# Four heads' compressed probabilities turned by one transpose and laid on a block diagonal by GpSimd's transfers

## The chip, the core and the metric

The kernel runs on one core of a Trainium2 chip. TensorE (PE) multiplies and transposes, and writes only to PSUM; VectorE (DVE) and ScalarE (ACT) read PSUM and do the element-wise work; SyncE (SP) issues nearly all transfers; GpSimd (POOL) has three short instructions. Each engine works through its own list in order and waits for the others on semaphores. The metric is the time of one execution on the device in microseconds, the median of several runs.

## The reference

One transformer layer on 512 positions of width 1024: half a SwiGLU feed-forward, a mixer, half a SwiGLU, a last norm. Half of the mixer's heads are sliding-window heads; the other half (two groups `g` of four heads `r`) add three branches: attention to all selected blocks, to a window, and to 31 compressed blocks of 32 positions. The compressed branch, cut to what matters:

```python
kc = compress_blocks(kc_raw, ck_pos, ck_w1, ck_b1, ck_w2)
vc = compress_blocks(vc_raw, cv_pos, cv_w1, cv_b1, cv_w2)
s = einsum('btgrd,bcgd->bgrtc', q, kc) * ATTN_SCALE
s = where(mask_c, s - slopes * dist_c, NEG_INF)
p_cmp = where(mask_c, softmax(s), 0.0)
o_cmp = einsum('bgrtc,bcgd->btgrd', p_cmp, vc)
...
return g0 * o_cmp + g1 * o_slc + g2 * o_win
```

Everything is float32. The kernel splits each operand into a high part (rounded) and a low part (the rest) and multiplies the parts, so every matrix that PE reads comes as two.

## The kernel before

The attention is a list of stages (class `Swa` for the sliding heads, class `Nsa` for the others), each for one group `g`, one block `i` of 128 queries and, in `Nsa`, one branch `br`. `attend` interleaves the scores of one stage with the outputs of the stage before it, and fills in between with pieces of other work (`fillers`: projections, and from the last block on `mix_out`, the output projection, lines 216 to 218 of the PE list). A stage's scores end with the normalisation: `tensor_scalar` on the probabilities `p` (line 1127, every second or third head on ACT), and last of all `tensor_tensor` on the compressed probabilities `self.c` (line 1131), a tile of 128 queries by 4 heads by 32 blocks.

Eight of the stages have a compressed part: per group one with `br == 0` (`i == 0`, where all branches are one stage) and three with `br == 2`. They are called compressed stages 1 to 8 here, in order of time. In their outputs, `transposed` turns the probabilities of each block of 128 keys: four PE transposes (one for each head) into one PSUM bank, an ACT copy for the high part (line 996) and a DVE subtraction for the low part (line 997). `times_values` does so for two blocks ahead and multiplies the turned blocks by the values (lines 1030 and 1031, PSUM bank `pv`). The compressed part is the last piece of that list: four transposes of 128 by 32 into 32 rows, a copy and a subtraction of 32 by 512, written to rows 0 to 31 of a tile `ct` whose other rows are zero, and two matmuls against `CV`, whose rows 0 to 31 hold the compressed values of the group and whose other rows are zero. `CV` is made once, in `network_o(1)` (lines 895 and 896).

The list of each engine is not simply the order of the code: the framework places the instructions of a stage by its own estimate of when they are ready. Tiles with four or fewer buffers (PSUM's `mm`) are reused in turn. The names in the traces: `mm`, `sc`, `pv` are PSUM banks, `u` the tiles of high and low parts, `small` the tile that holds `self.c`, `cv` is `CV`.

Of the kernel before, what the change touches and what calls it, by code (L numbers as in the profile page):

```python
# [10 lines left out]
F32R = mybir.dt.float32r  # L11
BF16 = mybir.dt.bfloat16
AF = mybir.ActivationFunctionType
ALU = mybir.AluOpType
AX = mybir.AxisListType

P = 128
# [29 lines left out]
def tile_hybrid(ctx, tc, xT, f1_wi, f1_wo, wm_t, wm_n, cw1, cw2, small, wm_oa, wm_ob, wm_oc, f2_wi, f2_wo, const, out):  # L47
    nc = tc.nc
    V, A, PE = nc.vector, nc.scalar, nc.tensor

    sb = ctx.enter_context(tc.tile_pool(name="sb", bufs=1))
    psp = ctx.enter_context(tc.tile_pool(name="psp", bufs=1, space=bass.MemoryType.PSUM))

    def f(ap):
        return ap.bitcast(F32)

    def ps(tag="mm"):
        return psp.tile([P, 512], F32, tag=tag, name=tag, bufs=NB[tag])
# [8 lines left out]
    def flat(dt=F32R):  # L67
        return sb.tile([P, 1024], dt, tag="u", name="u", bufs=NU)

    def unit(dt=F32R):  # L70
        return flat(dt).rearrange("p (a t) -> p a t", a=2)
# [4 lines left out]
    def tmp():  # L76
        return sb.tile([P, 512], F32, tag="tmp", name="tmp", bufs=NTMP)
# [16 lines left out]
    ident = sb.tile([P, P], F32, tag="ident", name="ident")  # L94
# [708 lines left out]

    CV = sb.tile([P, 2, 2, HD], F32R, tag="cv", name="cv")
    ct = unit()
    zero = ones.unsqueeze(1).to_broadcast([P, 4, P])
    A.activation(CV.rearrange("p g a d -> p (g a d)").rearrange("p (a t) -> p a t", t=P), zero[:, :2], AF.Copy, scale=0.0)
    for a in range(2):  # L810
        A.activation(ct[:, a, :].rearrange("p (a t) -> p a t", t=P), zero, AF.Copy, scale=0.0)

# [57 lines left out]
    def network_o(kv):  # L870
        hT, w2 = state["hT", kv]
        po = ps()
        if kv == 0:
            for c in range(2):
                PE.matmul(po[:HD, :62], w2[:, c, :], hT[:, c, :], start=c == 0, stop=c == 1)
            kc = tmp()
            V.memset(kc[:HD, :64], 0.0)
            V.tensor_copy(
                kc[:HD, :64].rearrange("p (g c) -> p g c", g=2)[:, :, :NCMP],
                po[:HD, :62].rearrange("p (g c) -> p g c", g=2),  # L880
            )
            for g in range(2):
                put_key(kc[:HD, g * 32 : g * 32 + 32], 0, KT[g][0][:, 512:544], KT[g][1][:, 512:544])
        else:
            vc = tmp()
            V.memset(vc[:32, :128], 0.0)
            for g in range(2):
                for c in range(2):
                    PE.matmul(
                        po[:NCMP, g * HD : (g + 1) * HD], hT[:, c, g * NCMP : (g + 1) * NCMP], w2[:, c, :],  # L890
                        start=c == 0, stop=c == 1,
                    )
            V.tensor_copy(vc[:NCMP, :128], po[:NCMP, :128])
            vcv = vc[:32, :128].rearrange("p (g d) -> p g d", g=2)
            A.copy(CV[:32, :, 0, :], vcv)
            V.tensor_tensor(CV[:32, :, 1, :], vcv, f(CV[:32, :, 0, :]), op=ALU.subtract)
        yield 0.6


# [4 lines left out]
    def put_key(src, g, k1, k2):  # L904

        own = slice(g * HD, (g + 1) * HD)
        oth = slice((1 - g) * HD, (2 - g) * HD)
        A.copy(k1[own], src)
        V.tensor_tensor(k2[own], src, f(k1[own]), op=ALU.subtract)
        nc.sync.dma_start(f(k1[oth]), f(k1[own]))  # L910
        nc.sync.dma_start(f(k2[oth]), f(k2[own]))

    def keys(b, kind):
        o = ps()
        yield from proj(b, o)
        if kind == "b":
            SK.extend([unit(), unit()])
        elif not KT:
            for _ in range(2):
                k12 = double(F32R)  # L920
                KT.append([k12[:, :1056], k12[:, 1056:]])
        kz = tmp()
        V.tensor_tensor(kz, o, state["bc"], op=ALU.mult)
        for g in range(2):
            rows = slice(g * HD, (g + 1) * HD)
            if kind == "b":
                put_key(kz[rows, :], g, SK[0][:, g, :], SK[1][:, g, :])
            else:
                c = 544 if kind == "w" else 0
                put_key(kz[rows, :], g, KT[g][0][:, c : c + 512], KT[g][1][:, c : c + 512])  # L930


    VT = []
# [54 lines left out]
    def small_t(n, name):  # L988
        return sb.tile([P, n], F32, tag="st" + name, name=name, bufs=3)

    def transposed(pl, rows, cols):
        pt = ps()
        for r in range(4):
            PE.transpose(pt[:rows, r * P : (r + 1) * P], pl[r][:, cols], ident)  # L994
        u = unit() if rows == P else ct
        A.copy(u[:rows, 0, :], pt[:rows, :])
        V.tensor_tensor(u[:rows, 1, :], pt[:rows, :], f(u[:rows, 0, :]), op=ALU.subtract)
        return u

    def put_o(pv, kb0, i):  # L1000
        low = tmp()
        A.copy(low[lo, :], pv[hi, :])
        pvv = pv.rearrange("p (a two t) -> p a two t", a=2, two=2)
        lov = low.rearrange("p (a two t) -> p a two t", a=2, two=2)
        ob = tmp()[:, :256].rearrange("p (a t) -> p a t", a=2)
        for par in range(2):
            V.tensor_tensor(ob[par * HD : (par + 1) * HD], pvv[lo, :, par, :], lov[lo, :, par, :], op=ALU.add)
        ts = slice(i * P, (i + 1) * P)
        for a in range(2):
            if OB[kb0 + a] is None:  # L1010
                OB[kb0 + a] = unit()
            u = OB[kb0 + a]
            A.copy(u[:, 0, ts], ob[:, a, :])
            V.tensor_tensor(u[:, 1, ts], ob[:, a, :], f(u[:, 0, ts]), op=ALU.subtract)

    def times_values(work, pv, first, last):


        pairs = [work[n : n + 2] for n in range(0, len(work), 2)]
        ahead = []  # L1020
        for n in range(len(pairs) + 1):
            cur = []
            if n < len(pairs):
                cur = [(transposed(pl, rows, cols), rows, v) for pl, cols, rows, v in pairs[n]]
                if n == 0:
                    yield 0.44 * len(cur)
            for m, (u, rows, v) in enumerate(ahead):
                a = first and n == 1 and m == 0
                b = last and n == len(pairs) and m == len(ahead) - 1
                PE.matmul(pv, v, u[:, 0, :], start=a, stop=False)  # L1030
                PE.matmul(pv, v, u[:, 1, :], start=False, stop=b)
                yield 0.43 + 0.44 * len(cur) / len(ahead)
            ahead = cur

    class Nsa:
# [98 lines left out]
        def outputs(self):  # L1134
            g, i, br = self.g, self.i, self.br
            if br != 2:
                state["pv"] = ps("pv")
            pv = state["pv"]

            def values_of(b, kb):  # L1140
                return VT[b][:, kb, g].rearrange("p a d -> p (a d)")

            if br == 0:
                work = [(self.p, slice(b * P, (b + 1) * P), P, values_of(b, 0)) for b in range(2)]
            else:
                work = [(self.p, slice(kb * P, (kb + 1) * P), P, values_of(br - 1, kb)) for kb in range(i + 1)]
            if br != 1:
                cl = [self.c[:, r, :] for r in range(4)]
                work.append((cl, slice(0, 32), 32, CV[:, g].rearrange("p a d -> p (a d)")))
            yield from times_values(work, pv, br != 2, br != 1)  # L1150
            if br != 1:
                put_o(pv, g * 2, i)

    class Swa:
# [41 lines left out]
        def outputs(self):  # L1196
            g, i, W, c0 = self.g, self.i, self.W, self.c0
            pv = ps("pv")
            work = [
                (self.p, slice(n * P, (n + 1) * P), P, VT[2][:, c0 // P + n, g].rearrange("p a d -> p (a d)"))  # L1200
                for n in range(W // P)
            ]
            yield from times_values(work, pv, True, True)
            put_o(pv, 4 + g * 2, i)
# [68 lines left out]
    kb, vals = keys(8, "b"), values()  # L1273
# [15 lines left out]
    piece("c1", compressed(1))  # L1289
    piece("kw", keys(3, "w"))  # L1290
    piece("o0", network_o(0))
    piece("n1", network(1))
    piece("q4", queries(4))
    piece("q5", queries(5))
    piece("o1", network_o(1))
    piece("q6", queries(6))
    piece("q7", queries(7))
# [122 lines left out]
```

## Time and profile before

| | |
|---|---|
| median of 3 runs | 972.47 us (972.42 to 972.49) |
| the profiled execution | 973.86 us, its span 972.1 us |
| PE busy | 957.3 us (98%) |
| DVE busy | 814.3 us (84%) |
| ACT busy | 633.2 us (65%) |
| POOL busy | 3.5 us |

The span is the time from the first to the last recorded instruction; what lies around it is the difference to the execution's time. Matmuls are pipelined, so the recorded duration of one is longer than its distance to the next; what one costs in a dense stretch is read from the distance of starts. The compressed stages lie between about 478 and 603 us.

### The profile page before, as it was taken

To read this page: it belongs to the slowest core of one execution; us is meant where nothing else is said; L and a number is where in the kernel's file an instruction comes from. 1 tells how busy PE (TensorE), PEld (TensorE's weight loads), DVE (VectorE), ACT (ScalarE), POOL (GpSimd) and SP (SyncE) were. 2 spreads that over 40 slices of the span, in tenths; PEclk is the share of its full clock that TensorE was granted. 3 is DMA by queue.
4 is the path that set the end of the run, shared out by engine and by line. 5 is a ranking of instruction groups with operands and counts; after the bars stand their busy time and mean duration, and the time that the engine had idled before them with its cause. 6 is when DMAs were issued, how large, how long until landed. Compare 5 with 4: busy or idle time off the path is not lost.

```text
span 972.1 us, 13619 instructions
## 1 busy us (share of the span) xinstructions
PE 957.3 (98%) x5008; PEld 809.8 (83%) x5008; DVE 814.3 (84%) x1442; ACT 633.2 (65%) x1273; POOL 3.5 (0%) x7
## 2 busy tenths in 40 slices
PE   9999999999999999999999999999999999999996
PEld 7888888888888889888777888888888888888886
DVE  6999879888798675788899999999987988879864
ACT  7786676665766545554777785768667666676654
POOL 0000000000000000000000000000000000000000
PEclk9999999999999999999999999999999999999999
DMA  8133314233124313122410212223331323312122
GB/s 317 55 130 130 142 43 141 77 119 140 46 77 172 111 45 109 44 91 84 137 44 5 83 44 70 93 75 115 126 141 44 140 77 120 134 51 94 50 64 86
DMA packets 36386, 93.98 MB, mean 97 GB/s; under 512 B 4448, under 2 KB 8928, under 8 KB 36320
## 3 DMA queue, kind: packets, MB, share of 16 engines
q1 hardware_dynamic: 35648, 92.82, 27.7%
q8 instruction: 39, 0.64, 0.3%
q10 hardware_dynamic: 672, 0.30, 0.1%
q14 instruction: 27, 0.22, 0.1%
HBM read 89.40 MB, written 2.10 MB: 94 GB/s over the span
## 4 chain that ended last, share of the span: by engine, by line
PE 88%; DVE 6%; ACT 2%; DMA 2%; issue 1%; POOL 0%; SPq 0%; ACTq 0%; DVEq 0%
PE mm L352 18%; PE mm L353 9%; PE sc L352 7%; PE mm L218 4%; PE mm L216 4%; PE mm L217 4%; PE sc L353 4%; PE pv L441 4%; PE pv L443 3%; PE sc L441 3%; PE sc L442 3%; PE pv L442 3%; PE sc L443 3%; PE mm L994 2%; PE mm L850 2%; DMA t<-in_f_wi_dram 1%
## 5 line engine op out<-in xcount | busy, mean ns | idle before, releaser
L352 PE MATMUL mm<-u 128*128 128x512 f32 x760 | 273.7, 396 | 0.2 <-ACT mm L625 0.2
L353 PE MATMUL mm<-u 128*128 128x256 f32 x760 | 211.3, 279 | 0.0
L352 PEld LDWEIGHTS mm<-u 128*128 128x128 f32 x760 | 142.5, 188 | 34.6 <-DVE tmp L643 0.8
L353 PEld LDWEIGHTS mm<-u 128*128 128x128 f32 x760 | 143.2, 188 | 6.1
L352 PE MATMUL sc<-u 128*128 128x512 f32 x304 | 110.7, 396 | 0.0
L216 PE MATMUL mm<-u 128*128 128x512 f32 x220 | 87.7, 399 | 0.5 <-ACT u L104 0.5
L218 PE MATMUL mm<-u 128*128 128x512 f32 x220 | 86.4, 393 | 0.3 <-DVE u L105 0.3
L217 PE MATMUL mm<-u 128*128 128x512 f32 x220 | 86.4, 393 | 0.0
L353 PE MATMUL sc<-u 128*128 128x256 f32 x304 | 85.0, 280 | 0.0
L352 PEld LDWEIGHTS sc<-u 128*128 128x128 f32 x304 | 57.1, 188 | 13.2
L405 DVE TENSOR_TENSOR u<-tmp,u 128x512 fp32r<-128x512 f32 (+1 forms) x96 | 60.6, 641 | 8.0 <-ACT u L404 7.9
L404 ACT CAST u<-tmp 128x512 fp32r<-128x512 f32 (+1 forms) x96 | 54.7, 585 | 18.6 <-PE sc L443 13.6
L617 ACT COPY tmp<-mm 128x256 f32<-128x256 f32 x76 | 28.4, 374 | 50.5 <-PE mm L353 50.5
L353 PEld LDWEIGHTS sc<-u 128*128 128x128 f32 x304 | 57.2, 188 | 3.0
L441 PE MATMUL pv<-u 128*128 128x512 f32 x144 | 57.3, 398 | 0.0
L441 PE MATMUL sc<-u 128*128 128x512 f32 x144 | 57.1, 397 | 0.0
L443 PE MATMUL pv<-u 128*128 128x512 f32 x144 | 56.9, 395 | 0.0
L442 PE MATMUL sc<-u 128*128 128x512 f32 x144 | 56.7, 394 | 0.0
L442 PE MATMUL pv<-u 128*128 128x512 f32 x144 | 56.6, 393 | 0.0
L443 PE MATMUL sc<-u 128*128 128x512 f32 x144 | 56.2, 390 | 0.0
L330 DVE TENSOR_TENSOR u<-t,u 128x1024 fp32r<-128x1024 f32 x38 | 46.4, 1222 | 4.9 <-ACT u L327 3.0
L218 PEld LDWEIGHTS mm<-u 128*128 128x128 f32 x220 | 41.3, 188 | 9.3 <-DVE u L105 1.2
(266 smaller groups left out, 2258.5 us busy)
## 6 DMA issues: line engine op xcount, KB each, us to landing
t<-in_f_wi_dram SPq DMA_DIRECT2D x87, 512.0 KB, 4.4
tmp<-in_f_wo_dram SPq DMA_DIRECT2D x80, 256.0 KB, 4.7
t<-in_wm_t_dram SPq DMA_DIRECT2D x13, 512.0 KB, 4.3
t<-in_cw_dram SPq DMA_DIRECT2D x8, 512.0 KB, 4.3
h<-in_xT_dram SPq DMA_DIRECT2D x4, 512.0 KB, 8.1
tmp<-in_f_wo_dram SPq DMA_DIRECT2D x16, 128.0 KB, 4.3
t<-in_wm_oa_dram SPq DMA_DIRECT2D x4, 512.0 KB, 3.8
t<-in_wm_n_dram SPq DMA_DIRECT2D x4, 408.0 KB, 5.9
```

The lines of the kernel that those rows point to most:

```text
L216: PE.matmul(o, wh[:, c], xs[k][:, 0, :], start=s0, stop=False)
L217: PE.matmul(o, wh[:, c], xs[k][:, 1, :], start=False, stop=False)
L218: PE.matmul(o, wl[:, c], xs[k][:, 0, :], start=False, stop=s1)
L330: V.tensor_tensor(wl, t[:, 0:1024], f(wh), op=ALU.subtract)
L352: PE.matmul(o, w[0][:, c], x[k], start=new, stop=False, skip_group_check=not first)
L353: PE.matmul(o[:, :256], w[1][:, c], x[k][:, 0], start=False, stop=k == 3, skip_group_check=not first)
L404: A.copy(u[:, 0, :n], raw[:, :n])
L405: V.tensor_tensor(u[:, 1, :n], raw[:, :n], f(u[:, 0, :n]), op=ALU.subtract)
L441: PE.matmul(o, wh[:, c], u[:, 0, :], start=False, stop=False, skip_group_check=True)
L442: PE.matmul(o, wh[:, c], u[:, 1, :], start=False, stop=False, skip_group_check=True)
L443: PE.matmul(o, wl[:, c], u[:, 0, :], start=False, stop=q == j1 - j0 - 1, skip_group_check=True)
L617: A.copy(z, o[:, t2])
```

## The change

`transposed_c` takes the place of `transposed` for the compressed part. It turns the whole tile of 128 queries by 4 heads by 32 blocks with one PE transpose, so that head `r` comes out in rows 32 r to 32 r + 31. ACT and DVE make the two parts in one tile `cparts` of 128 by 2 by 128. Then four GpSimd transfers, one for each head, copy 32 rows of both parts to `ct`, each to its own rows and to its own 128 columns; `ct` is zero elsewhere. The matmul against `CV` thus meets each head in other rows, and `CV` gets the same 32 rows four times: three SP transfers after line 896 replace the zeroing of `CV` at the start. `transposed_c` is called where the list of work is built, before the stage's other transposes.

```diff
--- before.py
+++ after.py
@@ -803,10 +803,11 @@
 
 
 
+
     CV = sb.tile([P, 2, 2, HD], F32R, tag="cv", name="cv")
     ct = unit()
+    cparts = sb.tile([P, 2, P], F32R, tag="cparts", name="cparts")
     zero = ones.unsqueeze(1).to_broadcast([P, 4, P])
-    A.activation(CV.rearrange("p g a d -> p (g a d)").rearrange("p (a t) -> p a t", t=P), zero[:, :2], AF.Copy, scale=0.0)
     for a in range(2):
         A.activation(ct[:, a, :].rearrange("p (a t) -> p a t", t=P), zero, AF.Copy, scale=0.0)
 
@@ -894,6 +895,8 @@
             vcv = vc[:32, :128].rearrange("p (g d) -> p g d", g=2)
             A.copy(CV[:32, :, 0, :], vcv)
             V.tensor_tensor(CV[:32, :, 1, :], vcv, f(CV[:32, :, 0, :]), op=ALU.subtract)
+            for r in range(1, 4):
+                nc.sync.dma_start(f(CV[r * 32 : r * 32 + 32]), f(CV[:32]))
         yield 0.6
 
 
@@ -988,14 +991,26 @@
     def small_t(n, name):
         return sb.tile([P, n], F32, tag="st" + name, name=name, bufs=3)
 
-    def transposed(pl, rows, cols):
+    def transposed(pl, cols):
         pt = ps()
         for r in range(4):
-            PE.transpose(pt[:rows, r * P : (r + 1) * P], pl[r][:, cols], ident)
-        u = unit() if rows == P else ct
-        A.copy(u[:rows, 0, :], pt[:rows, :])
-        V.tensor_tensor(u[:rows, 1, :], pt[:rows, :], f(u[:rows, 0, :]), op=ALU.subtract)
+            PE.transpose(pt[:, r * P : (r + 1) * P], pl[r][:, cols], ident)
+        u = unit()
+        A.copy(u[:, 0, :], pt)
+        V.tensor_tensor(u[:, 1, :], pt, f(u[:, 0, :]), op=ALU.subtract)
         return u
+
+    def transposed_c(c):
+
+        pt = ps()[:, :P]
+        PE.transpose(pt, c.rearrange("p r c -> p (r c)"), ident)
+        u = cparts
+        A.copy(u[:, 0, :], pt)
+        V.tensor_tensor(u[:, 1, :], pt, f(u[:, 0, :]), op=ALU.subtract)
+        for r in range(4):
+            rows = slice(r * 32, r * 32 + 32)
+            nc.gpsimd.dma_start(f(ct[rows, :, r * P : (r + 1) * P]), f(u[rows]))
+        return ct
 
     def put_o(pv, kb0, i):
         low = tmp()
@@ -1021,10 +1036,10 @@
         for n in range(len(pairs) + 1):
             cur = []
             if n < len(pairs):
-                cur = [(transposed(pl, rows, cols), rows, v) for pl, cols, rows, v in pairs[n]]
+                cur = [(pl if cols is None else transposed(pl, cols), v) for pl, cols, v in pairs[n]]
                 if n == 0:
                     yield 0.44 * len(cur)
-            for m, (u, rows, v) in enumerate(ahead):
+            for m, (u, v) in enumerate(ahead):
                 a = first and n == 1 and m == 0
                 b = last and n == len(pairs) and m == len(ahead) - 1
                 PE.matmul(pv, v, u[:, 0, :], start=a, stop=False)
@@ -1141,12 +1156,11 @@
                 return VT[b][:, kb, g].rearrange("p a d -> p (a d)")
 
             if br == 0:
-                work = [(self.p, slice(b * P, (b + 1) * P), P, values_of(b, 0)) for b in range(2)]
+                work = [(self.p, slice(b * P, (b + 1) * P), values_of(b, 0)) for b in range(2)]
             else:
-                work = [(self.p, slice(kb * P, (kb + 1) * P), P, values_of(br - 1, kb)) for kb in range(i + 1)]
+                work = [(self.p, slice(kb * P, (kb + 1) * P), values_of(br - 1, kb)) for kb in range(i + 1)]
             if br != 1:
-                cl = [self.c[:, r, :] for r in range(4)]
-                work.append((cl, slice(0, 32), 32, CV[:, g].rearrange("p a d -> p (a d)")))
+                work.append((transposed_c(self.c), None, CV[:, g].rearrange("p a d -> p (a d)")))
             yield from times_values(work, pv, br != 2, br != 1)
             if br != 1:
                 put_o(pv, g * 2, i)
@@ -1197,7 +1211,7 @@
             g, i, W, c0 = self.g, self.i, self.W, self.c0
             pv = ps("pv")
             work = [
-                (self.p, slice(n * P, (n + 1) * P), P, VT[2][:, c0 // P + n, g].rearrange("p a d -> p (a d)"))
+                (self.p, slice(n * P, (n + 1) * P), VT[2][:, c0 // P + n, g].rearrange("p a d -> p (a d)"))
                 for n in range(W // P)
             ]
             yield from times_values(work, pv, True, True)
```

How the PE list changes around compressed stage 2 (`g` 0, `i` 1, `br` 2): from the stage's first transposes to its matmul against `cv`. `small_3277` is the tile of compressed probabilities. Before:

```order
L216 MATMUL mm<-u 128x512
L994 MATMUL mm<-ident,tmp 128x128 x8
L994 MATMUL mm<-ident,small_3277 32x128 x4
L985 MATMUL sc<-t_3949,u 128x416
L986 MATMUL sc<-t_3949,u 128x416
L1030 MATMUL pv<-u 128x512
...
L1030 MATMUL pv<-u 128x512
L985 MATMUL sc<-t_3949,u 128x416
L1031 MATMUL pv<-u 128x512
L1030 MATMUL pv<-u,cv 128x512
L986 MATMUL sc<-t_3949,u 128x416
```

And now, where lines 997, 1006, 1045 and 1046 are the old 994, 994, 1030 and 1031:

```order
L218 MATMUL mm<-u 128x512
L1006 MATMUL mm<-ident,small_3277 128x128
L997 MATMUL mm<-ident,tmp 128x128 x8
L988 MATMUL sc<-t_3949,u 128x416
...
L1079 MATMUL sc<-u 128x32
L1076 MATMUL sc<-u 128x384
L997 MATMUL mm<-ident,tmp 128x128 x3
L1045 MATMUL pv<-u,cv 128x512
L1046 MATMUL pv<-u,cv 128x512
```

One transpose stands ahead of the eight others in place of four behind them; three transposes of the next stage and all scores have moved ahead of the matmul against `cv`.

The DVE list of the same stage, from the normalisation of the compressed probabilities on, before:

```order
L1131 TENSOR_TENSOR small_3277<-small_3277,su 128x128
L978 TENSOR_TENSOR u<-tmp,u 64x512
L105 TENSOR_TENSOR u<-t_4351,u 128x1024
L1057 TENSOR_REDUCE nm<-sc 128x1
L997 TENSOR_TENSOR u<-mm,u 128x512 x2
L1057 TENSOR_REDUCE nm<-sc 128x1
L997 TENSOR_TENSOR u<-mm,u 32x512
```

And now (line 1009 is the subtraction in `transposed_c`):

```order
L1146 TENSOR_TENSOR small_3277<-small_3277,su 128x128
L981 TENSOR_TENSOR u<-tmp,u 64x512
L105 TENSOR_TENSOR u<-t_4351,u 128x1024
L1072 TENSOR_REDUCE nm<-sc 128x1
L1009 TENSOR_TENSOR cparts<-mm,cparts 128x128
L1000 TENSOR_TENSOR u<-mm,u 128x512 x2
```

The subtraction for the compressed part stands where the first subtraction of the other blocks stood, behind the same three instructions.

POOL's list now:

```order
L197 ISA
L197 TENSOR_TENSOR rcol<-rc,mhalf 128x4 x2
L1012 DMA u<-cparts 32x2x128 x32
L197 TENSOR_TENSOR rcol<-rc,mhalf 128x4
L1429 UNCONDITIONAL_BRANCH
```

The 32 transfers, four for each compressed stage, are all that stands there between the second and the third of its computing instructions.

## Rows read from the trace of the kernel before

**Rows 1.** Windows: busy time by engine, granted clock, DMA share, in three stretches:

```profile
478.00:603.00 125.00, 122.37 (x676) 101.21 (x675) 114.66 (x288) 97.70 (x295) 0.00 (x0) 1.00 0.15 52
...
966.00:968.00 2.00, 0.00 (x0) 0.00 (x0) 1.44 (x4) 1.02 (x2) 0.00 (x0) 1.00 1.01 367
968.00:970.00 2.00, 0.00 (x0) 0.00 (x0) 0.00 (x0) 0.00 (x0) 0.00 (x0) 0.77 0.69 230
```

**Rows 2.** Groups by line and shape from 478 to 603: busy, mean ns, idle before:

```profile
L997 DVE TENSOR_TENSOR u<-mm,u 128x512 fp32r<-128x512 f32 x42 | 27.7, 682 | 2.0 <-ACT u L996 1.8
...
L1127 DVE TENSOR_SCALAR tmp<-tmp,su 128x512 f32<-128x512 f32 x12 | 5.1, 482 | 0.0
...
L997 DVE TENSOR_TENSOR u<-mm,u 32x512 fp32r<-32x512 f32 x8 | 5.3, 666 | 0.0
...
L996 ACT CAST u<-mm 32x512 fp32r<-32x512 f32 x8 | 4.5, 566 | 0.5 <-PE mm L994 0.5
...
L1013 ACT CAST u<-tmp 128x128 fp32r<-128x128 f32 x16 | 4.0, 300 | 1.9 <-DVE tmp L1007 1.9
L1014 DVE TENSOR_TENSOR u<-tmp,u 128x128 fp32r<-128x128 f32 x16 | 4.0, 285 | 0.1
...
L1127 DVE TENSOR_SCALAR tmp<-tmp,su 128x256 f32<-128x256 f32 x12 | 3.5, 341 | 0.0
```

**Rows 3.** Timeline, PE: start, duration, line, tile, shape, count:

```profile
489.07 0.60 PE L994 MATMUL mm<-ident,small 128*32 128x128 f32 x4
...
522.01 0.40 PE L216 MATMUL mm<-u 128*128 128x512 f32 x1
522.24 0.39 PE L217 MATMUL mm<-u 128*128 128x512 f32 x1
```

**Rows 4.** Timeline, DVE, after the second compressed stage's normalisation:

```profile
500.94 0.28 DVE L1131 TENSOR_TENSOR small<-small,su 128x128 f32<-128x128 f32 x1
501.25 0.69 DVE L978 TENSOR_TENSOR u<-tmp,u 64x512 fp32r<-64x512 f32 x1
501.98 1.23 DVE L105 TENSOR_TENSOR u<-t,u 128x1024 fp32r<-128x1024 f32 x1
503.12 0.55 DVE L1057 TENSOR_REDUCE nm<-sc 128x1 f32<-128x384 f32 x1
503.59 1.28 DVE L997 TENSOR_TENSOR u<-mm,u 128x512 fp32r<-128x512 f32 x2
```

**Rows 5.** Timeline, DVE, the same two lines in the first and eighth stage:

```profile
488.62 0.28 DVE L1131 TENSOR_TENSOR small<-small,su 128x128 f32<-128x128 f32 x1
...
489.51 0.69 DVE L997 TENSOR_TENSOR u<-mm,u 128x512 fp32r<-128x512 f32 x1
...
594.45 0.28 DVE L1131 TENSOR_TENSOR small<-small,su 128x128 f32<-128x128 f32 x1
...
595.76 0.69 DVE L997 TENSOR_TENSOR u<-mm,u 128x512 fp32r<-128x512 f32 x1 [0.43 <-ACT u L996]
```

**Rows 6.** Timeline, POOL, two of its three computing instructions:

```profile
25.81 1.26 POOL L197 TENSOR_TENSOR rcol<-rc,mhalf 128x4 f32<-128x4 f32 x1 [25.37 <-ACT rc L194]
360.02 1.01 POOL L197 TENSOR_TENSOR rcol<-rc,mhalf 128x4 f32<-128x4 f32 x1 [332.95 <-ACT rc L194]
```

**Rows 7.** DMA issues: tile, queue, count, KB each, us from issue to landing:

```profile
u<-u SPq DMA_DIRECT2D x4, 128.0 KB, 2.3
...
tmp<-in_cw_dram SPq DMA_DIRECT2D x2, 64.0 KB, 1.9
```

**Rows 8.** Line 842: the same weight load's issue, ns min/median/max:

```profile
L842 SPq DMA_DIRECT2D tmp<-in_cw_dram x2: 327/328/328, 419.2 to 446.1; - x2
```

**Rows 9.** Tile cv: ns min/median/max, first and last start:

```profile
L1030 PE MATMUL pv<-u,cv x8: 393/395/496, 491.3 to 600.1; 128*128 128x512 f32 x8
...
L896 DVE TENSOR_TENSOR cv<-tmp,cv x1: 280/280/280, 479.3 to 479.3; 32x128 fp32r<-32x128 f32 x1
```

**Rows 10.** Timeline, SP queue, the weight loads around that time:

```profile
475.60 27.96 SPq L117 DMA_DIRECT2D t<-in_wm_oa_dram  x3
```

## The prediction

> **What bounds the kernel now.** I read the busy times first, then the windows around the compressed stages, then the groups by shape there, then the timelines of PE and DVE in single stages, and last every row on POOL and on transfers. The window from 478 to 603 us holds all eight compressed stages: PE is busy for 122.37 of 125.00 us and DVE for 114.66, ACT for 97.70, POOL for nothing [rows 1]. PE sets the end, and DVE is close behind it. So a PE instruction that disappears is worth its distance in PE's queue, and a PE instruction that must wait costs its whole wait, since everything behind it, filler work too, stands in the same queue. What PE loses now is 125.00 - 122.37 = 2.6 us in the whole stretch.
>
> **The transposes.** Each compressed stage loses three of its four small transposes. The four of a stage take 0.60 us from first start to last end, one alone 0.27, so their starts are (0.60 - 0.27) / 3 = 0.11 us apart [rows 3]. 8 stages x 3 x 0.11 = 2.6 us, all of it on PE. The one that is left has 128 columns of weights instead of 32 but the same 128 moving columns; I take it at 0.11 as well.
>
> **The copies.** ACT's 32x512 copy (566 ns) becomes one of 128x128 (300 ns), DVE's 32x512 subtraction (666 ns) one of 128x128 (285 ns) [rows 2]: 8 x 0.27 = 2.1 us less on ACT, 8 x 0.38 = 3.0 us less on DVE. Neither is the bound, so this can only shorten PE's waits. Of the 2.6 us of waits I give back half, 1.3 us; the bounds are 0 and 2.6.
>
> **Edits at nothing.** The zeroing of CV falls in the program's start, where ACT waits for the first loads. The three SP transfers that fill CV can start after 479.6 (479.3 + 0.28), and the first matmul that reads CV starts at 491.3 [rows 9]; three SP transfers of the nearest kind land in about 2.3 us each [rows 7], so some 9 us are left over. On SP they stand between weight loads, which are spread there over 27.96 us [rows 10]: nothing is queued close behind. Without that cover they would cost the first stage only.
>
> **The transfers.** This is the term that decides. Until now the low part went from DVE straight to PE. Now, between the two, POOL issues four transfers one after another, and the matmul against `cv` waits for all four. Call N the time from the end of DVE's subtraction to the landing of the fourth: a hand-over of 0.1 us, three issue distances, and the fourth's issue to landing. The trace before has no POOL transfer, so both are bounded. Issue distance: at least that of SP's cheapest, 0.33 us [rows 8]; at most that of POOL's longest instruction, 1.26 [rows 6]. The nearest row in engine is POOL's 1.01 us for an operation on only 4 columns, nearly all of it fixed cost. I take 0.8, the middle of the two ends, on POOL's side. Landing: 1.9 us (64 KB from HBM) to 2.3 (128 KB inside SBUF) on SP [rows 7]; I take 2.2, nearer to the copy inside SBUF. So N is at least 0.1 + 3 x 0.33 + 1.9 = 3.0, at most 0.1 + 3 x 1.26 + 2.3 = 6.2, and 0.1 + 2.4 + 2.2 = 4.7 in my forecast.
>
> The Trainium skill (DMA: Bandwidth & Descriptors, Anatomy of one DMA — SWDGE (gpsimd) path) gives a GpSimd transfer about 2.0 us from end to end and calls the making of its descriptors small. If the four issues cost nothing, N would be 2.1 us by it, an estimate, and the sum below would come out as the first rival does; no run here shows it.
>
> **What covers N.** PE goes on with other work between the compressed transpose and the matmul against `cv`. I counted that work in the new PE list, with 0.23 us for a matmul of 512 columns and 0.11 for a transpose [rows 3], narrower matmuls by their width: 3.2, 4.1, 5.5, 7.9, 6.2, 5.2, 5.3 and 5.0 us in stages 1 to 8. But the subtraction is not made at once. It now stands in DVE's list where the first subtraction of line 997 stood. In stage 2, DVE ends the normalisation at 500.94 + 0.28 = 501.22 and reaches that place at 503.59, behind 0.69 + 1.23 + 0.55 us of other work [rows 4]; with its own 0.28 the parts are ready 2.65 us after the transpose could start. Stage 1: 489.51 - 488.90 + 0.28 = 0.9 [rows 5]. In stage 8 the same difference is 595.76 - 594.73 = 1.0 [rows 5], but nothing stands between any more, so 0.9 again. All eight, worked out in the same way: 0.9, 2.65, 3.5, 1.55, 2.25, 1.3, 1.5, 0.9. Cover less this delay leaves 2.3, 1.45, 2.0, 6.35, 3.95, 3.9, 3.8 and 4.1 us for N.
>
> PE's wait at the matmul is N less what is left, where positive. For N = 4.7: 2.4 + 3.25 + 2.7 + 0 + 0.75 + 0.8 + 0.9 + 0.6 = 11.4 us. For N = 3.0: 0.7 + 1.55 + 1.0 = 3.3. For N = 6.2: 3.9 + 4.75 + 4.2 + 0 + 2.25 + 2.3 + 2.4 + 2.1 = 21.9. What is queued behind the waiting matmul is the next stage's transposes and scores; ACT and DVE wait for those in turn, but use the time to clear their lists. That brings the later subtractions forward: what the delays have above 0.9 adds up to 7.35 us (1.75 + 2.6 + 0.65 + 1.35 + 0.4 + 0.6), and I take a third of it back for N = 4.7, 2.5 us, half for N = 6.2, 3.7 us, and nothing for 3.0.
>
> DVE's `tensor_scalar` of line 1127 grows by (482 - 341) / 256 = 0.55 ns a column, the subtractions by (682 - 285) / 384 = 1.03 [rows 2]: line 1127 runs at twice the rate. The Trainium skill (SBUF — State Buffer, SBUF: two separate sides) says that while DVE is in such a two-port mode, GpSimd is locked out of a shared port and cannot write the descriptors of its transfers, and it advises against issuing them there; no run here shows a case of it. By that rule the three such instructions of the next stage that fall into the issue in stages 1 and 6, about 1 us in each, would add 2 us to the sum, 979.5; by the durations alone they add nothing, and I leave them out.
>
> **Sum.** -2.6 (transposes) - 1.3 (waits given back) + 11.4 (new waits) - 2.5 (lists cleared) = +5.0 us. The profiled execution took 973.86 us with a span of 972.1; 973.86 + 5.0 = 978.9. That execution is 1.4 us above the median of the runs, 972.47, so for the median I forecast 977.5 us.
>
> **Rivals.**
>
> *The transfers are hidden.* If POOL issues as fast as SP's cheapest and they land in 1.9 us, N = 3.0 and the sum is -2.6 - 1.3 + 3.3 = -0.6, 971.9; if N is under 1.5, no stage waits and it is -3.9, 968.6. For it: SP's rows [rows 7, 8], and that the scheduler put up to 7.9 us of work in between. Against it: POOL's 1.01 us for next to nothing [rows 6], and DVE's late place in stages 2 and 3 [rows 4]. It fails from about N = 3.2 on, where the new waits (0.9 + 1.75 + 1.2 = 3.9) eat the gain.
>
> *Gain and wait cancel.* N = 3.8 (issue distance 0.5, landing 2.2): 1.5 + 2.35 + 1.8 = 5.65 of waits, less 2.6, 1.3 and 0.5 for lists cleared, +1.3 us: 973.7.
>
> *The clock falls.* If the issue takes its upper bound, PE stands for up to 4.75 us at a time. The granted clock is 1.00 through the whole stretch, and at the end of the program, after PE has stopped, still 1.00 in 966 to 968 and 0.77 in 968 to 970 [rows 1]. Three waits of 3.9 to 4.75 us (stages 1 to 3) that each brought the lower level for as long as the wait would lose half of 12.85 us, 6.4, on top of 21.9 - 2.6 - 1.3 - 3.7 = 14.3: 993. Against it: it needs the upper bound first, and no wait of before is that long. [...]
>
> That the change does not do what it says I exclude: the new lists show one transpose in place of four and 32 transfers on POOL.
>
> **How the numbers follow.** Forecast 0.58, hidden 0.20, cancelled 0.16, clock 0.06. A measurement of this kernel can tell about 0.2% from no change, 1.9 us: below 970.5 is faster, above 974.4 slower. Of the hidden case's 968.6 to 971.9 I put 0.15 below 970.5 and 0.05 above. Of the cancelled case, 0.12 lies within, 0.04 above. The forecast's own range goes from 974 to 987 (972.47 + 14.3); I put 0.02 of it within. So faster 0.15, same 0.19, slower 0.66. The range of 970.0 to 986.5 holds the forecast, the cancelled case and half of the hidden one, and leaves out the clock and the far end of the hidden case.
>
> **What would show it.** Right: POOL rows of 32 transfers about 0.8 us apart; PE idle before the first matmul on `cv` in stages 1, 2 and 3 of 2 to 3 us each, put down to a DMA; none in stage 4; PE's busy time down by some 2.6 us in the small transposes and the window from 478 to 603 about 5 us longer; the rest of the program as before. Wrong: transfers 0.3 us apart, or landing under 1.5 us, would make the first rival; a clock under 1.00 between 480 and 610, the third. If PE waits for the DVE's subtraction or for a PSUM bank instead, in places that this list does not name, the cover was counted wrongly.

## The result, and the profile after

The changed kernel takes 980.87 us (median, 980.03 to 981.31) against 972.47 us (972.30 to 972.53) of the kernel before, run by turns on one chip: ratio 1.0085, 95% interval 1.0074 to 1.0097. It is slower by 8.4 us. The profiled execution took 980.87 us with a span of 978.5.

The loss lies in the mixer alone. GpSimd's `rcol` of line 197 stands once before the mixer's input and once behind the compressed stages; in the kernel before they start at 360.02 [rows 6] and 626.14, 266.1 us apart. First the row of before, then the changed kernel (timelines, POOL; start, duration, engine, line; in brackets the idle time ahead and what ended it):

```profile
626.14 1.01 POOL L197 TENSOR_TENSOR rcol<-rc,mhalf 128x4 f32<-128x4 f32 x1 [265.10 <-ACT rc L194]
```

```profile
358.73 1.01 POOL L197 TENSOR_TENSOR rcol<-rc,mhalf 128x4 f32<-128x4 f32 x1 [332.16 <-ACT rc L194]
489.00 2.39 POOL L1012 DMA_DIRECT2D u<-cparts  x4 [129.25 <-DVE cparts L1009]
505.19 2.12 POOL L1012 DMA_DIRECT2D u<-cparts  x4 [13.80 <-DVE cparts L1009]
...
632.65 1.03 POOL L197 TENSOR_TENSOR rcol<-rc,mhalf 128x4 f32<-128x4 f32 x1 [29.51 <-ACT rc L194]
```

They are 273.9 us apart, 7.8 more; the other 0.6 lie outside the recorded span, which is 2.4 us shorter than the execution here and 1.8 before. Four transfers take POOL 2.12 us. The instructions on the tile `cparts` (ns min/median/max), and the two new kinds of transfer (tile, queue, count, KB, us from issue to landing):

```profile
L1012 POOL DMA_DIRECT2D u<-cparts x32: 536/536/706, 489.0 to 602.6; - x32
L1008 ACT CAST cparts<-mm x8: 254/266/267, 488.1 to 600.1; 128x128 fp32r<-128x128 f32 x8
L1009 DVE TENSOR_TENSOR cparts<-mm,cparts x8: 279/284/292, 488.4 to 600.4; 128x128 fp32r<-128x128 f32 x8
...
DMA to landing us min/median/max: 1.7/1.7/4.4
```

```profile
u<-cparts POOLq DMA_DIRECT2D x32, 32.0 KB, 1.7
cv<-cv SPq DMA_DIRECT2D x3, 32.0 KB, 1.9
```

The windows that answer to [rows 1] (busy time of PE, PEld, DVE, ACT and POOL, granted clock, DMA share, GB/s):

```profile
478.00:603.00 125.00, 116.28 (x616) 94.33 (x615) 106.52 (x279) 89.98 (x288) 17.05 (x32) 0.99 0.16 53
505.00:510.00 5.00, 3.09 (x14) 2.14 (x14) 4.27 (x11) 1.69 (x5) 2.12 (x4) 1.00 0.70 236
600.00:605.00 5.00, 5.00 (x25) 4.68 (x24) 3.06 (x5) 3.48 (x7) 2.12 (x4) 0.66 0.12 26
```

PE now stands for 8.7 of the 125 us, where it stood for 2.6. PE, DVE and ACT all work less in the same time: none of them is fuller than before, and they wait for each other. PE's list of waits from 470 to 640 us (who waited for whom: us in total, times, longest):

```profile
PE mm L1006 <- DVE small L1146: 2.6, 3, 2.3
PE pv L1045 <- DMA u<-cparts: 1.4, 1, 1.4
PE sc L988 <- ACT tmp L1073: 1.4, 4, 0.8
PE pv L1046 <- DVE u L1000: 1.0, 3, 0.6
PE pv L1045 <- ACT u L999: 0.9, 1, 0.9
PE pv L1045 <- DVE tmp L1022: 0.7, 1, 0.7
PE pv L1045 <- issue: 0.3, 1, 0.3
PE sc L988 <- ACT small L1073: 0.2, 1, 0.2
PE mm L997 <- DVE tmp L1142: 0.2, 1, 0.2
```

Only 1.4 of these 8.7 us are put down to a transfer. The two largest single waits, in PE's timeline:

```profile
510.25 0.47 PE L1045 MATMUL pv<-u,cv 128*128 128x512 f32 x1 [1.43 <-DMA u<-cparts]
...
597.15 0.39 PE L218 MATMUL mm<-u 128*128 128x512 f32 x1
599.80 0.31 PE L1006 MATMUL mm<-ident,small 128*128 128x128 f32 x1 [2.26 <-DVE small L1146]
599.94 3.58 PE L997 MATMUL mm<-ident,tmp 128*128 128x128 f32 x16
```

The first is stage 2, where weight loads fill the DMA engines (share 0.70 in 505 to 510) and a landing takes 4.4 us. The second is stage 8: the compressed transpose, now first, waits for the normalisation. In PE's list nothing stands between `L218` and that transpose, and on DVE the normalisation stands behind a subtraction that needs the product of this same `L218` (timeline, DVE):

```profile
597.58 0.69 DVE L1229 TENSOR_TENSOR h<-mm,h 128x512 f32<-128x512 f32 x1 [0.48 <-PE mm L218]
598.18 1.27 DVE L1142 TENSOR_SCALAR tmp<-tmp,su 128x512 f32<-128x512 f32 x3
599.37 0.28 DVE L1146 TENSOR_TENSOR small<-small,su 128x128 f32<-128x128 f32 x1
```

Behind this wait the granted clock fell to the lower of its two levels, 1.2 GHz: 16 transposes took 3.58 us, where 15 distances of 0.11 [rows 3] and one duration of 0.27 (the median of `L994` before) are 1.9. That is 1.7 us more. What stayed open is how 1.4 us of landing become a loss of 8.4.

### The profile page after: what moved, and what is told of

It reads as the page before. It is cut to its first block, busy times and chain, and to the rows that moved or that the text cites. A ratio compares the mean times of both kernels' runs of the same rounds, so it can differ in the third digit from the quotient of the medians.

```text
span 978.5 us, 13659 instructions
## 1 busy us (share of the span) xinstructions
PE 958.0 (98%) x4984; PEld 809.7 (83%) x4984; DVE 812.6 (83%) x1442; ACT 630.6 (64%) x1272; POOL 21.0 (2%) x39
## 4 chain that ended last, share of the span: by engine, by line
PE 89%; DVE 6%; ACT 2%; DMA 1%; issue 1%; POOL 0%; ACTq 0%; DVEq 0%
PE mm L352 18%; PE mm L353 9%; PE sc L352 7%; PE mm L218 4%; PE mm L216 4%; PE mm L217 4%; PE sc L353 4%; PE pv L441 3%; PE pv L443 3%; PE sc L441 3%; PE sc L442 3%; PE pv L442 3%; PE sc L443 3%; PE sc L218 2%; PE sc L217 2%; PE sc L216 2%
## 5 line engine op out<-in xcount | busy, mean ns | idle before, releaser
L218 PE MATMUL mm<-u 128*128 128x512 f32 x220 | 86.2, 392 | 0.3 <-DVE u L105 0.3
L218 PEld LDWEIGHTS mm<-u 128*128 128x128 f32 x220 | 41.3, 188 | 9.2 <-DVE u L105 0.7
```

The costliest lines, as they stand in the source:

```text
L218: PE.matmul(o, wl[:, c], xs[k][:, 0, :], start=False, stop=s1)
```

## The experiments

Each was timed in turns with the kernel before on its chip (972.1 to 972.8 us there). In the diffs, `-` is the changed kernel's line, unless said. "List" is the order in which the framework lays out one engine's instructions; the profile records 4,984 of TensorE's in every kernel with one transpose. N is the prediction's time from the end of the subtraction to the last piece in its place.

**Without the transfers.** The compressed branch adds nothing here.

```
-        for r in range(4):
-            rows = slice(r * 32, r * 32 + 32)
-            nc.gpsimd.dma_start(f(ct[rows, :, r * P : (r + 1) * P]), f(u[rows]))
```

> The changed kernel without the 32 GpSimd transfers: the turned parts are made but never laid into ct, so the compressed branch adds nothing to the output; all matmuls are still made. Theory A (the transfers' landing is what costs, as predicted): the whole loss goes and the 2.6 us of transposes come out, 969 to 971 us. Theory B (the place costs: the compressed transpose stands first and waits for the normalisation, its copies stand ahead of the others'): only the 2.1 us go for which the changed kernel's PE stands at the matmul against cv, 978 to 979 us. Theory C (the clock drop behind the 2.4 us wait in stage 8 is the larger part): 1.7 us or so depend on whether that wait is still there.

971.31 us, ratio 0.9986 (0.9977 to 0.9996): 1.5 us faster than before, and just above theory A's range. So the whole loss, 9.6 us between this kernel and the changed one, comes with the transfers and what depends on them; the first place by itself does not make it.

**At the old place.** The transpose stands behind the others of its stage again, with its transfers.

```
-                work.append((transposed_c(self.c), None, CV...))     # first
+                work.append((self.c, None, CV...))                   # transposed in its turn
```

> The changed kernel with the compressed transpose back at its old place, behind the other transposes of its stage, transfers by GpSimd as now. Theory A: the cover shrinks to 2 to 3.5 us against a chain of copy, subtraction and 3.4 us of transfers, some 1.5 to 2.5 us of wait in each of eight stages, 984 to 990 us. Theory B: the waits for the normalisation and for the late copies go (5 to 6 us), the new waits at cv are the same as in A; about 980 to 984 us.

984.02 us, 1.0112 (1.0097 to 1.0127): 3 us worse than the changed kernel, at the edge of both expectations, so it does not tell A from B. Part of the 3 us is the clock, which in its profile falls further (granted 0.97 in 478 to 603, where the changed kernel has 0.99). Its waits (whole program) say DMA for 1.3 us, and more elsewhere:

```profile
PE mm L997 <- DVE tmp L1142: 5.1, 6, 1.4
...
PE pv L1045 <- DMA u<-cparts: 1.3, 1, 1.3
```

**The first place alone**, in the kernel before: its four small transposes come ahead of the others.

```
-                work.append((cl, slice(0, 32), 32, CV...))                     # line of the kernel before
+                work.append((transposed(cl, 32, slice(0, 32)), None, 32, CV...))
```

> The kernel before with only the place changed: its four small transposes, the 32x512 copy and subtraction come first in the stage instead of last; no transfers. Theory A: 972 to 973 us, as before. Theory B: PE waits for the normalisation in stages 1, 5 and 8 and for the other blocks' copies, 976 to 979 us.

974.18 us, 1.0014 (1.0005 to 1.0023). The place costs 1.4 us here (0.5 to 2.2), between the two expectations.

**Transfers issued by SP.**

```
-            nc.gpsimd.dma_start(
+            nc.sync.dma_start(
```

> The changed kernel with its 32 transfers issued by SP in place of GpSimd. SP's issue of such a transfer took 0.57 to 0.59 us (cv), landing 1.9, so N = 0.1 + 3 x 0.58 + 1.9 = 3.7 against 0.1 + 3 x 0.54 + 1.7 = 3.4 us. Theory A: about 0.3 us more in each stage that waits, and more where weight loads stand in SP's list ahead of them, 981 to 984 us. Theory B: the same as the changed kernel within 1 us, 980 to 982 us.

978.29 us, 1.0055 (1.0039 to 1.0072). That is below both expectations. An issue takes SP 592 ns (median) against POOL's 536 and the landing is 1.9 us, so N is no shorter (3.9 in most stages), and yet the kernel is 2.6 us faster than the changed one; why is open. The loss is of the same kind (PE's waits from 470 to 640 us, in the slowest of four executions, 979.88):

```profile
PE mm L1006 <- DVE small L1146: 4.0, 3, 2.3
...
PE pv L1045 <- DMA u<-cparts: 0.5, 2, 0.3
```

The longest is again the one at stage 8, with the clock falling behind it.

**No transfers, narrow pieces.** ScalarE and VectorE write the four blocks of the diagonal themselves; the rows keep their partitions, so nothing needs to cross. First at the old place, then first of the stage.

```
-            nc.gpsimd.dma_start(f(ct[rows, :, r * P : (r + 1) * P]), f(u[rows]))
+            A.copy(u[rows, 0, c], pt[rows])                                # u = ct, c = block r
+            V.tensor_tensor(u[rows, 1, c], pt[rows], f(u[rows, 0, c]), op=ALU.subtract)
```

> One transpose of the four heads, at the old place (behind the other transposes of the stage), and no transfers: eight 32x128 copies and subtractions, four on ScalarE and four on VectorE, write the blocks of the diagonal themselves. If the loss lies in the transfers (their waits and what hangs on them): 966 to 972 us, since eight pieces of some 0.25 us on two engines stand against a copy of 0.57 and a subtraction of 0.67. If the narrow pieces on ScalarE and VectorE cost as much as the transfers, since both engines are late for the value multiplications: 975 us or more.

> The same with the one transpose first of its stage. If the first place costs about what four transposes ahead of the others cost the kernel before (+1.4 us), this is 1 to 2 us above the version at the old place; if the first place is free once nothing waits for a transfer, as the version without transfers says (971.3 us), it is equal to it within 0.5 us or up to 1 us faster.

985.14 us (1.0117 to 1.0147) and 979.92 us (1.0060 to 1.0094). The first is the second branch of its expectation; the second is in neither branch of its own, as the first place is 5.2 us better here. A loss as large comes without any transfer, so a transfer is not needed for one. But the pieces have a price of their own (with the transpose first DVE is busy for 820.3 us and ACT for 638.0, in the changed kernel 812.6 and 630.6), and the pair cannot say what the transfers cost. The second kernel has the same wait at the same place, 2.3 us for the normalisation ahead of `L1006` of stage 8, and the clock falls there too: that wait needs no transfer. (Its lists are not the changed kernel's: over a hundred of TensorE's rows stand elsewhere.)

**All transfers made, none waited for.** The value multiplications of the compressed branch read `VT[0]` in place of the tile that the transfers fill.

```
-        return ct
+        return VT[0].rearrange(...)        # read in place of ct
```

> All 32 transfers are made, but the compressed branch's value multiplications read stored values (VT[0]) in place of the tile that the transfers fill, so nothing on TensorE depends on a transfer, and TensorE's list is that of the version without transfers. If the transfers cost by the wait on their landing and by the order that this dependence gives the lists: 971 to 972.5 us, as without transfers. If they cost by being there (GpSimd's issues beside VectorE, traffic beside the weight loads): 975 us or more, up to the 980.9 of the changed kernel.

971.30 us, 0.9990 (0.9980 to 0.9999), as without transfers, and the lists of TensorE, ScalarE and VectorE are those of that kernel row for row. 32 issues and 1 MB of traffic cost nothing that can be told (971.30 against 971.31 us). What costs is that TensorE depends on them.

**One transfer of four** (three heads add nothing).

```
-        for r in range(4):
+        for r in range(1):
```

> Only the first of the four transfers of a stage is made (three heads add nothing), so the last landing stands about 1.6 us earlier, 3 issues of 0.54 us; the dependence stays. If the loss is sized by the time from the subtraction to the last landing: the two direct waits (0.33 and 1.43 us) are gone and the time is 975 us or less. If the order that the dependence gives the lists costs, TensorE's list here is near that of the version without transfers and the time is 971 to 974. If any transfer that TensorE waits for costs the whole amount: 979 to 981.

973.79 us, 1.0015 (1.0005 to 1.0024), in the first two of its three ranges, so it does not tell size from order. One wait for the transfer, with the fall of the clock behind it, is enough for the 2.5 us against the kernel without transfers (timeline, PE; windows as above; the profiled execution took 974.46):

```profile
505.09 0.39 PE L218 MATMUL mm<-u 128*128 128x512 f32 x1
507.55 0.79 PE L1045 MATMUL pv<-u,cv 128*128 128x512 f32 x1 [2.06 <-DMA u<-cparts]
```

```profile
504.00:507.00 3.00, 1.48 (x8) 0.95 (x6) 2.93 (x9) 0.67 (x2) 0.00 (x0) 1.00 0.82 320
507.00:511.00 4.00, 3.46 (x13) 3.15 (x14) 1.25 (x5) 2.17 (x6) 0.00 (x0) 0.57 0.00 0
```

It is stage 2 again: with 320 GB/s on the way, weights nearly all of it, this landing takes 4.1 us where six others take 1.7 to 1.9 (stage 4: 2.8), and the clock falls behind the wait. Elsewhere a shorter N leaves nothing to wait for.

**GpSimd copies in place of transfers, once and twice.** This pair lengthens N without changing the order. GpSimd itself copies the four pieces, 0.44 us each. N becomes 1.8 us in every stage, or 3.6 to 4.6 with each copy made twice, and the framework keeps the lists of the kernel without transfers: all rows with single copies, all but one of TensorE's with double. The changed kernel's list is another: 247 of its rows stand elsewhere.

```
-            nc.gpsimd.dma_start(f(ct[rows, :, r * P : (r + 1) * P]), f(u[rows]))
+            nc.gpsimd.tensor_copy(ct[rows, :, r * P : (r + 1) * P], f(u[rows]))
+            nc.gpsimd.tensor_copy(ct[rows, :, r * P : (r + 1) * P], f(u[rows]))    # second kernel only
```

> The four transfers of a stage are replaced by four copies that GpSimd itself makes, 32 x 2 x 128, onto the same blocks of the diagonal (the rows keep their partitions, so no transfer is needed). The value multiplications read the tile as in the changed kernel, but the lists of TensorE, ScalarE and VectorE are, row for row, those of the version without transfers, not those of the changed kernel (247 of 4,872 rows of TensorE's list stand elsewhere there). If the changed kernel loses by the order of its lists: 971 to 973 us, plus a wait in stages 1 and 2 if four copies take over 2 us. If it loses by the time from the subtraction to the last piece, whatever the order: by four copies of 0.4 to 0.6 us this is 2 to 2.5 us against 3.4 of the transfers, so 976 to 978.

> The same with each of the four copies made twice, which doubles the time from the subtraction to the last piece to some 3.2 to 5 us (about the 3.4 of the transfers or more), with the lists of TensorE, ScalarE and VectorE still those of the version without transfers (one row of TensorE's apart). If the loss is the order: above the single copies only by what their direct waits at the value multiplications grow, 1 to 3 us in stages 1 and 2, so 973 to 976. If the loss is the time to the last piece: 980 or more, as the changed kernel.

971.37 us, 0.9993 (0.9983 to 1.0002), and 978.59 us, 1.0069 (1.0054 to 1.0084). PE's waits from 470 to 640 us with single copies:

```profile
PE sc L988 <- ACT small L1073: 0.7, 2, 0.5
PE pv L1046 <- DVE u L1000: 0.7, 2, 0.4
PE mm L1006 <- DVE small L1146: 0.6, 1, 0.6
PE mm L997 <- DVE tmp L1142: 0.6, 1, 0.6
PE mm L997 <- DVE cparts L1009: 0.5, 1, 0.5
```

and with double copies:

```profile
PE pv L1046 <- POOL u L1013: 5.2, 6, 1.4
PE mm L1006 <- DVE small L1147: 0.8, 2, 0.6
PE mm L997 <- DVE tmp L1143: 0.8, 1, 0.8
PE sc L988 <- ACT small L1074: 0.7, 2, 0.5
PE pv L1047 <- DVE u L1000: 0.7, 2, 0.4
PE mm L997 <- DVE cparts L1009: 0.5, 1, 0.5
```

The single copies came out in the range of the order theory, the double copies between the two ranges. Neither expectation had the cover in this order right: with single copies the first multiplication against `cv` starts 2.0 to 7.1 us behind the end of the subtraction, so an N of 1.8 is hidden in every stage. With one order, 1.8 to 2.8 us more of N cost 7.2 us. The profile puts 5.2 of it at the place that the prediction had named, that first multiplication; by its distance from the end of the subtraction, which grows in seven of the eight stages, it is 6.6. The other five rows stand nearly as they were. The added copies also hold up DVE, by 0.2 us in each of five instructions, too little to be the loss. PE's waits are 8.7 us in all, 3.1 with single copies, and 8.7 in the changed kernel too, spread over nine places there. The granted clock is 1.00 in 470 to 640 us in both kernels of this pair. The order theory, as I had it (the loss is the order, N costs 1 to 3 us), is refuted: a long N costs this much in this order too. In the same order, stage 8 waits for the normalisation for 0.64 us only (single copies; ten multiplications stand between the `L218` that it needs and the transpose), and the 16 transposes behind it take 1.91 us:

```profile
592.72 0.30 PE L1006 MATMUL mm<-ident,small 128*128 128x128 f32 x1 [0.64 <-DVE small L1146]
```

**GpSimd copies at the old place.**

```
-                work.append((transposed_c(self.c), None, CV...))     # first, with GpSimd copies
+                work.append((self.c, None, CV...))
```

> GpSimd's four copies (4 x 0.44 = 1.76 us as measured), with the one transpose at its old place, behind the other transposes of the stage. If the time from the subtraction to the last piece against the work that covers it decides: the cover of the old place is smaller by the transposes that no longer stand behind it (0.6 to 1.7 us a stage), so waits of up to 1 us come in several stages and the time is 973 to 977. If the first place itself costs (+1.4 us in the kernel before): 970 to 971.

978.23 us, 1.0060 (1.0045 to 1.0075): a little over its range. The old place leaves less work ahead of the multiplication: PE waits for POOL 5.5 us in seven stages, 2.5 of it in stage 8, where POOL was held up (timelines of POOL and DVE):

```profile
583.73 1.75 POOL L1012 CAST u<-cparts 32x256 fp32r<-32x256 f32 x4 [16.62 <-DVE cparts L1009]
600.69 3.57 POOL L1012 CAST u<-cparts 32x256 fp32r<-32x256 f32 x4 [15.21 <-DVE cparts L1009]
```

```profile
600.54 1.21 DVE L105 TENSOR_TENSOR u<-t,u 128x1024 fp32r<-128x1024 f32 x1
...
602.28 1.27 DVE L105 TENSOR_TENSOR u<-t,u 128x1024 fp32r<-128x1024 f32 x1
```

**Two queues.** SP and GpSimd issue by turns: N = 0.3 + 0.6 + 1.9 = about 2.8 us, half of the transfers on either queue.

```
-            nc.gpsimd.dma_start(
+            (nc.gpsimd if r % 2 else nc.sync).dma_start(
```

> The changed kernel with the four transfers of a stage issued by turns by SP and by GpSimd, so two issues follow each other on a queue in place of four: 0.1 + 0.57 + 1.8 = about 2.5 us from the subtraction to the last landing, where four on one queue take 3.4. If the time to the last piece decides, between the points measured so far (1.8 us: 971.4; 3.4 to 3.5 us: 978.6 to 980.9): 973.5 to 976.5. If any transfer in the way costs the whole amount, through the lists' order: 978 or more.

974.98 us, 1.0025 (1.0015 to 1.0034), as expected from N. PE's waits (whole program, in the slowest of ten executions, 976.07):

```profile
PE mm L1006 <- DVE small L1146: 2.9, 3, 1.8
...
PE pv L1045 <- DMA u<-cparts: 0.9, 2, 0.4
```

In one view, for the kernels with the transpose first:

| tile filled by | N, us: most stages; longest | time, us | wait at `cv` for the filler, us |
|---|---|---|---|
| nothing, or not read | none | 971.3, 971.3 | 0 |
| GpSimd, four copies | 1.8; 1.8 | 971.4 | 0 |
| one transfer | 2.0; 4.5 in stage 2 | 973.8 | 2.1, stage 2 |
| two queues | 2.8; 5.6 in stage 2 | 975.0 | 0.9 |
| GpSimd, eight copies | 3.6; 4.6 in stage 5 | 978.6 | 5.2 |
| four transfers, GpSimd | 3.6; 5.2 in stage 2 | 980.9 | 1.4 |
| four transfers, SP | 3.9; 5.3 in stage 2 | 978.3 | 0.5 |

The time rises with N, but not strictly: SP's longer N costs less than GpSimd's. Only the rows with copies, and those where nothing is read, share one order.

## Why the prediction was right, and where it was not

The forecast was 977.5 us in a range of 970.0 to 986.5, slower with 0.66. The time came out at 980.9 and the deciding cause was named: the time from the subtraction to the last landing, against the work that covers it. The sizes of its terms were wrong in both directions, and that the sum still came within 3.4 us is in part luck: too long an N stands against returns that did not come.

*N.* Predicted 0.1 + 3 x 0.8 + 2.2 = 4.7. Measured: the subtraction of stage 1 ends at 488.68 (488.39 + 0.29) and the first issue starts at 489.00, so the hand-over is 0.3; issues stand 0.53 apart; the landing takes 1.7. N = 3.6 us in five stages, near the lower bound, 3.9 in stage 1, 4.4 in stage 7 and 5.2 in stage 2, where a landing takes up to 4.4. I had put the issue distance on the side of POOL's 1.01 us for an operation on 4 columns [rows 6]; SP's 0.33 [rows 8] was nearer. The landing fell below its lower bound of 1.9 [rows 7] in most stages. The Trainium skill (DMA: Bandwidth & Descriptors, Anatomy of one DMA — SWDGE (gpsimd) path) gives some 2.0 us from end to end. The 1.7 us here agree roughly; the estimate of 2.1 for N made from it does not, since four issues on one queue follow each other.

*The new waits.* By the prediction's own scheme, N = 3.6 in every stage would have cost 1.3 + 2.15 + 1.6 = 5.1 us of waits and the sum would have been about +0.8, next to the rival in which gain and wait cancel; with the N of each stage it is 1.6 + 3.8 + 1.6 + 0.6 = 7.6, and +3.7 before anything is given back. The step that failed is "ACT and DVE ... use the time to clear their lists", with its -2.5: nothing is cleared. From the start of the compressed transpose to the end of its subtraction every stage takes the same time with double copies as with single ones, within 0.03 us, though PE waits 5.6 us longer; in the changed kernel, in another order, stages 3 to 5 take 0.4 to 1.5 us more. The cover was counted too large for the later stages as well: double copies still wait 1.23 us in stage 5 and 1.44 in stage 6, where 3.95 and 3.9 us, counted in the changed kernel's list, were to cover N (POOL needed 4.5 and 3.8 us there):

```profile
555.10 0.50 PE L1046 MATMUL pv<-u,cv 128*128 128x512 f32 x1 [1.23 <-POOL u L1013]
...
570.72 0.50 PE L1046 MATMUL pv<-u,cv 128*128 128x512 f32 x1 [1.44 <-POOL u L1013]
```

*Where the waits are.* I expected 2 to 3 us in each of stages 1 to 3 before the first matmul on `cv`. There is 0.33 in stage 1, 1.43 in stage 2, none in stage 3 and, as forecast, none in stage 4. What came instead is a sign that the prediction had listed as one of being wrong: PE waits for DVE in places that it does not name, and so, by its own rule, the cover was counted wrongly. In the changed kernel the framework moves other work in front of that matmul; that the wait for the transfers turns up at that work is my reading, and no run shows it wait by wait. PE's 8.7 us of waits are 5.6 more than with single copies; with the 1.7 us of the clock this makes 7.3 of the 9.5 us between the two kernels. Of the other 2.2 us, 0.6 lie outside the spans (978.5 and 969.6) and 1.6 are not assigned. That about the same N costs 7.2 us in the other order shows that a long N is enough for most of the loss. It does not clear the order: the wait of 2.26 us in stage 8, 1.6 more than with single copies, follows from what that order puts next to each other and comes without transfers too (narrow pieces, first), and the clock's 1.7 us hang on it. Whether the changed kernel's order would cost this much with a short N was not tried.

*DVE's place.* In stage 2 the subtraction starts 2.64 us behind the start of the normalisation's last instruction (501.97, 504.61), where 2.65 had been worked out from [rows 4]; right. DVE's timeline:

```profile
501.97 0.28 DVE L1146 TENSOR_TENSOR small<-small,su 128x128 f32<-128x128 f32 x1
...
504.61 0.28 DVE L1009 TENSOR_TENSOR cparts<-mm,cparts 128x128 fp32r<-128x128 f32 x1
```

*The gains.* The copies became 266 and 284 ns, where 300 and 285 had been taken from [rows 2]. Without the transfers PE is busy for 954.2 us, 3.1 less than before, near the forecast 2.6; in the changed kernel, slower clock included, for 958.0. But transposes and copies together were to bring 3.9 us where nothing waits, 968.6. The three kernels in which nothing waits for `ct` are 0.8 to 1.5 us faster than before, the 0.8 not clear of no change. If the first place costs one transpose the 1.4 us that it cost four, it takes these back, a price that the sum did not have; 1 to 1.7 us of the 3.9 did not come for reasons that no run separates.

*Edits at nothing.* CV's three transfers: right, they are done some 11 us before the first matmul that reads it (479.6 + 1.9, and 492.9).

*The rivals.* Hidden needed N up to 3.0; with N = 1.8 it is what the single copies show. The third rival's sign, a clock under 1.00 between 480 and 610, did come, once, but not by its mechanism: behind a wait of 2.26 us for the normalisation, at a price of 1.7 us, where the rival had three waits of 3.9 to 4.75 us for the transfers.

*GpSimd's port.* I left out the rule (the Trainium skill, SBUF — State Buffer, SBUF: two separate sides) by which VectorE can shut GpSimd out of a shared port. For issues it is worth little here: the one beside line 1142's instructions (the old 1127) took 0.62 us (490.76, stage 1) against 0.54, where the prediction had priced the rule at 2 us; with the transpose at the old place the longest took 0.80. (The longest of the changed kernel, 706 ns, is its first issue, with no such instruction beside it.) For GpSimd's own copies it is real: 3.57 against 1.75 us beside two VectorE subtractions with both operands in SBUF. The section names that case, two SBUF inputs against a GpSimd operation that reads SBUF, and the trace agrees.

## What to carry to other kernels

Between a producer and a full matmul queue, a relay over transfers is priced by the time to the last landing less the work that stands in between; in one order the runs show this nearly to the microsecond (6.6 of 7.2 us). A loss can be there even where the profile puts hardly any wait down to the transfer, since the scheduler lays out the lists anew when the dependence changes; how much of it is then the relay and how much the new order has to be tested. To do so, cut the dependence and keep the transfers, then lengthen the relay without changing the order. Where the rows keep their partitions, an idle engine can make the copies itself: here that takes 1.8 us in place of 3.6 and is 9.5 us faster than the changed kernel, though it does not beat the kernel before by more than can be told.

## What the hardware showed that I had not expected

- A landing of 32 KB from SBUF to SBUF took 1.7 us (median), and up to 4.4 us beside weight loads (236 GB/s in 505 to 510; 4.1 us at 320 GB/s with one transfer).
- The granted clock fell to the lower level behind waits of 2.06 us (one transfer, stage 2) and 2.26 us (changed kernel, stage 8), but not behind one of 2.54 us at 604.31 with the copies at the old place, where the clock in 604 to 610 is 1.00. What tells them apart stays open.
- GpSimd makes a copy of 32x256 words every 0.44 us when alone, and four take 3.57 us in place of 1.75 beside two 128x1024 subtractions of VectorE in SBUF.
